# Two of seven quarter products as wide products, and a tail with seeded banks: one change to a two-layer decoder trunk on Trainium2

## The chip, the cores and the metric

The kernel runs on one core of one Trainium2 chip. The metric is the device time of one execution in microseconds; less is better. The profile names the engines PE (TensorE, matrix products), PEld (its weight loads), DVE (VectorE), ACT (ScalarE), POOL (GpSimd) and SP (SyncE, which mainly issues DMAs).

## The reference

Two decoder layers over 512 tokens of width 1024, all in float32. Layer 0 mixes tokens with a gated delta rule, layer 1 with sliding-window attention; both also read 256 memory tokens, and both end with a feed-forward part. The change lies in that part and in the last norm:

```python
D_MODEL = 1024; SEQ = 512; DEPTH = 2; D_FF = 2816

def rms_norm(x, g):
    return x * rsqrt(mean(x * x, axis=-1) + EPS) * g

def swiglu(h, w_gate_up, w_down):
    gu = h @ w_gate_up                       # 1024 -> 2 x 2816
    return (silu(gu[..., :D_FF]) * gu[..., D_FF:]) @ w_down

for layer in range(DEPTH):
    ...                                      # token mixing, memory attention, w_out
    x = x + swiglu(rms_norm(x, ln_ffn[layer]), w_gate_up[layer], w_down[layer])
    ...
return rms_norm(x, ln_final)
```

## The kernel before, in words

Activations lie transposed in SBUF: a tile holds 128 features by 512 tokens, and the residual stream is the eight tiles `x[0]` to `x[7]`. Every float32 product is made of three fp32r matmuls: each operand is split into a rounded part (hi) and the rest (lo), and `mm3` adds wh·ah, wh·al and wl·ah in one PSUM bank. `split` makes the parts: ACT copies hi (`whi<-wraw`, `h<-x`), DVE subtracts (lo). `pair` allocates the two parts of an activation, `h` and `l`, as two tiles. A bank holds 128 x 512 floats, and `banks` deals the eight banks out by tag.

A tile scheduler walks the program in the order in which it is written and puts each instruction into the queue of its engine; each queue runs in order, and semaphores order the queues among each other. The generator `quarters` is advanced step by step by `begin` and `end`, so that the pieces of neighbouring pairs interleave.

**The feed-forward part.** `ffn` does the 22 gate and 22 up columns of 128 features in two halves of 11. Column 0 of each half, and gates 1 and 2 of the first half, are plain products 512 tokens wide. All others go in pairs through `quarters`: 19 pairs in each layer, 38 in all. A pair of columns is a 2 x 2 block matrix (two columns by two halves of the 1024 input features), the input another (two halves of the features by two halves of 256 tokens), and Strassen's scheme in Winograd's form makes the four output blocks of seven products in place of eight. Each product sums over four steps (512 features), each of three matmuls 256 tokens wide.

The products are called here by the input that they read. 11 reads the first feature half of the first 256 tokens, 21 and 22 the second feature half of the first and of the last 256 tokens, straight from the parts of `h`; t1 to t4 read sums that `token_sums` has made once. PE's order in a pair is 11, t1, t4 of the pair before, t2, 21, 22, t3. The banks are `pa`, `pb` and `pc`, of which 256 columns each are used: `pa` gathers 11, t2 (their sum is called u2) and t3 and t4 behind it; `pb` holds 21, `pc` t1 and on top of it 22. What is wanted between, ACT copies out of PSUM by `held` into `fs`: p1 (product 11), p5 (t1) and u2. DVE adds 21 to p1 and 22 to u2. Each product's weight quarter (`wraw` by DMA; the sums `ws`, of which s1 is one, by a DMA and an accumulating DMA of POOL) is split just before it is needed into a ring of six places (`ring`: three buffers of `whi` and `wlo`, two halves each).

**The down projection** follows each half: for m = 0 to 7 it sums eleven steps into a bank `pj`, and DVE adds that to `x[m]`.

**The tail** is the end of layer 1: output tiles m = 6 and m = 7 of the last down projection, each in two parts of 256 tokens. PE's order is m6a, m7a, m6b, m7b (a the first 256 tokens, b the last). After each product `add` puts it on `x[m]` by DVE and ACT squares the result into `sq`; `final` sums the squares over the features with matmuls by `ones` and takes the reciprocal root by ACT, once for a part; `store` scales the output tiles `T` by it and sends them off. Ahead of the products' results, ACT copies tiles 0 to 5 times their gain into `T` for both parts, twelve scalings of 128 x 256.

Of the kernel before, what the change touches and what calls it, by code (L numbers as in the profile page):

```python
# [18 lines left out]
P = 128  # L19
# [64 lines left out]
    return c  # L84


class Builder:
    def __init__(self, tc, a):
        self.tc, self.nc, self.a = tc, tc.nc, a
# [71 lines left out]

    def pair(self, pool, tag=None, bufs=None):
        if tag is None:
            tag, bufs = "", KD
        return tuple(self.t(pool, [P, T], F32R, tag + p, bufs) for p in "hl")


    def split(self, src, hi, lo, eng=None):
# [27 lines left out]
    def mm3(self, ps, w, k, act, start, stop, more=False):  # L196

        (wh, wl), (ah, al) = w, act
        s = slice(k * P, (k + 1) * P)
        self.head = self.mm(ps, wh[:, s], ah, start, False, more)  # L200
        self.mm(ps, wh[:, s], al, False, False, more)
        self.last = self.mm(ps, wl[:, s], ah, False, stop, more)

    def project(self, src, acts, tag="pj", order=range(KD), w=None):
        steps = self.projected(src, acts, tag, order, w)
# [38 lines left out]
    def build(self):  # L244
        tc, nc, a = self.tc, self.nc, self.a
        with ExitStack() as st:
            opened = lambda name, **kw: tc.tile_pool(name=name, bufs=1, reuse_waits="tile", **kw)
            pool = lambda name, **kw: st.enter_context(opened(name, **kw))
            cp = pool("const")
            self.wpool, self.apool = pool("w"), pool("acta")  # L250
            self.dpool = pool("scratch", space=DRAM)
            self.load_constants(cp)
            self.weng = nc.vector
            with opened("layer0", side="right") as self.mpool:
                with self.banks(pj=3, g=2, sc=3):
# [10 lines left out]
            with opened("ffn0", side="right") as fp, self.banks(pj=2, g=6):  # L266
                self.ffn(fp, xp, 0, h, self.apool, rope=True)
            with self.banks(pj=2, qk=2, pt=2), opened("swa", side="right") as sp:
                h = self.output(xp, 1, *self.swa(sp))
            with opened("ffn1", side="right") as fp, self.banks(pj=2, g=6):  # L270
                self.ffn(fp, xp, 1, h, self.bpool)

    def load_constants(self, cp):
# [820 lines left out]
    def ffn(self, fp, xp, layer, h, apool, rope=False):  # L1094
# [6 lines left out]
        col = lambda f, up: a["wgu"][layer, 2 * f + up]  # L1101

        def gate(f, up=()):
            ps = self.project(col(f, 0), h, "pj")
# [54 lines left out]
        for f0 in (0, half):  # L1159
            acts.clear()  # L1160
            places.clear()
            up = self.projected(col(f0, 1), h, "g")
            g = gate(f0, up)
            u = self.t(fp, [P, T], F32, "fu", 3)
            self.tt(nc.vector, u, list(up)[-1], g, ALU.mult)
            put(u)
            for f in range(f0 + 1, f0 + half, 2):
                if f == 1:
                    g = []
                    for i in range(2):  # L1170
                        for _ in range(2 - i):
                            sums.append(self.token_sums(fp, layer, len(sums), h))
                        g.append(gate(f + i))
                    sums.append(self.token_sums(fp, layer, len(sums), h))
                else:
                    g = begin(f, 0, (self.rstd, self.rstd), "fg", 4, lambda x: self.fn(x, x, AF.Silu))
                begin(f, 1, g, "fu", 3, put)
            end()
            self.acc = self.floor if layer else None
            tail = KD - 2 if f0 and layer else KD  # L1180
            down = lambda m, j, n, **kw: self.weight(a["wdn"][layer, m][:, (f0 + j) * P:(f0 + j + n) * P], **kw)
            for m in range(tail):
                if layer and f0 == 0:
                    self.tt(nc.vector, self.x[m], self.x[m], self.root, ALU.mult)
                ps = self.bank("pj")
                for j, n in ((0, 6), (6, 5)):
                    w = down(m, j, n)
                    for k in range(n):
                        self.mm3(ps, w, k, acts[j + k], j + k == 0, j + k == half - 1)
                add(self.x[m], ps)  # L1190
                if f0:
                    self.acc = self.accumulate(xp, self.acc, self.x[m], m)
                if rope and f0 == 0 and m == 0:
                    self.rope_tables(fp)
        if tail < KD:
# [9 lines left out]
            for t in parts:  # L1205
                acc = self.acc[:, t]
                for m in range(tail, KD):
                    ps = self.bank("pj")[:, t]
                    for k in range(half):
                        self.mm3(ps, w[m][k // 6], k % 6, [x[:, t] for x in acts[k]], k == 0, k == half - 1)  # L1210
                    x = self.x[m][:, t]
                    add(x, ps)
                    sq = self.t(fp, [P, T], F32, "fg", 4)[:, t]
                    self.square(sq, x)
                    if m < KD - 1:
                        self.copy(outs[len(ends)][1][:, m % 4, :], x, scale=self.gain(G_FIN, m))
# [3 lines left out]
                ends.append(self.final(fp, (acc, sq), t))  # L1220
            for n, ((ps, r), o, t) in enumerate(zip(ends, outs, parts)):
                self.store(ps, r, o, t, n)

    def token_sums(self, fp, layer, j, h):

# [19 lines left out]
        hl = self.weight(None, raw=raw, pool=fp, tags=("T", "T"), bufs=8)  # L1245
        parts = {f"t{i + 1}": [x[:, i * q:(i + 1) * q] for x in hl] for i in range(4)}
        parts["11"] = [x[:, :q] for x in h[j]]
        parts["21"], parts["22"] = ([x[:, i * q:(i + 1) * q] for x in h[j + 4]] for i in range(2))
        return parts

    def quarters(self, fp, src, sums, by, u, ring):
# [13 lines left out]
        ins = nc.sync.dma_start(last, a22).ins  # L1265
        if self.behind is not None:
            self.nosync(ins, self.behind)
        pa, pb, pc = (self.bank("g")[:, :q] for _ in range(3))

        def product(ps, raw, b, first):  # L1270

# [5 lines left out]
        def held(ps):  # L1277
            o = self.t(fp, [P, q], F32, "fs", 3)
            self.copy(o, ps)
            return o  # L1280

        product(pa, a1[:, :T], "11", True)
        p1 = held(pa)
        self.held = self.copied
        product(pc, s1, "t1", True)
        p5 = held(pc)
        yield

        self.tt(nc.vector, a1[:, :T], s1, a1[:, :T], ALU.add)
        product(pa, a1[:, :T], "t2", False)  # L1290
        u2 = held(pa)
        product(pb, a1[:, T:], "21", True)
        self.tt(nc.vector, u[0][:, :q], pb, p1, ALU.add)
        self.tt(nc.vector, a1[:, T:], a1[:, :T], a1[:, T:], ALU.add)
        product(pc, a1[:, T:], "22", False)
        self.tt(nc.vector, u[0][:, q:], pc, u2, ALU.add)
        self.tt(nc.vector, u[0], u[0], by[0], ALU.mult)
        product(pa, s3, "t3", False)
        self.stt(u[1][:, q:], pa, -1.0, p5, ALU.mult, ALU.subtract)
# [12 lines left out]

    def rstd_from(self, acc, *parts, after, root=None):
        self.use(LN_EXP)
        ps = self.bank("pt" if "pt" in self.pbufs else "g")
        self.sum_parts(ps, acc, *parts, after)
        if root is None:
            self.rsqrt(self.rstd, ps, D)
# [168 lines left out]
    def final(self, fp, squares, t):  # L1487

        self.use(ROOT)
        ps, to = (self.bank("g")[:, t] for _ in range(2))  # L1490
        for k, sq in enumerate(squares):
            self.mm(ps, self.ones, sq, k == 0, k == len(squares) - 1)
        r = self.t(fp, [P, T], F32, "ws", 4)[:, t]
# [1 line left out]
            self.fn(o, ps, AF.Abs_reciprocal_sqrt, scale=1.0 / D)  # L1495
        return to, r

    def store(self, ps, r, o, t, part):

        nc = self.nc  # L1500
        rows = self.a["out"][part]
# [1 line left out]
        wide = lambda f, n: f.unsqueeze(1).to_broadcast([P, n, t.stop - t.start])  # L1503
        send = lambda k, n, by=nc.sync: by.dma_start(rows[:, k:k + n, :], some(k, n))
        self.tt(nc.gpsimd, some(0, 2), some(0, 2), wide(r, 2), ALU.mult)
        for k, n in ((2, 2), (4, 3)):
            self.tt(nc.vector, some(k, n), some(k, n), wide(ps, n), ALU.mult)
            send(k, n)
        self.stt(some(7, 1)[:, 0, :], self.x[7][:, t], self.gain(G_FIN, 7), ps, ALU.mult, ALU.mult)
        send(7, 1)  # L1510
        send(0, 2, nc.scalar if part else nc.sync)


# [62 lines left out]
```

## Time and profile before

| | |
|---|---|
| runs | 1138.91, 1139.19, 1139.49 us; median 1139.19 |
| the profiled execution | 1139.24 us; its span from the first to the last instruction 1137.2 us |
| PE busy | 1127.4 us, 99% of the span, 7337 matmuls |
| DVE busy | 829.0 us, 73% |
| ACT busy | 634.1 us, 56% |
| POOL busy | 72.8 us, 6% |
| mean granted TensorE clock | 0.999 |

Busy shares are means over stages with different limits, and an engine with free time delays nothing unless something waits for it. In rows of the order of time the columns are start, length, engine, line, operation, tiles and shapes, with a wait and what ended it in brackets; "x4" at the end stands for four in a row.

### The profile page before, as it was taken

The page shows a single profiled execution, that of the slowest core. Times are in us where ns is not written, and L with a number is a line of the kernel's source. Part 1 is how long each engine was busy: PE and PEld are TensorE (multiplying, and loading weights), DVE is VectorE, ACT ScalarE, POOL GpSimd, SP SyncE. Part 2 cuts the span into 40 slices and gives each one's busy share as a digit, 9 for nine tenths or more (in the row PEclk, how much of TensorE's full clock was granted, in tenths as well). Part 3 has the DMA queues.
Part 4 walks back from the last instruction along what each step waited for, and adds up shares of the span by engine and source line. Part 5 has one row for each costly group of instructions (what it writes and reads, how often), then busy time and mean ns, then how long its engine had stood idle before and what let it go on. Part 6 is the DMA issues. An engine that isn't in the chain of part 4 may idle for free.

```text
span 1137.2 us, 19289 instructions
## 1 busy us (share of the span) xinstructions
PE 1127.4 (99%) x7337; PEld 991.3 (87%) x7337; DVE 829.0 (73%) x1542; ACT 634.1 (56%) x1271; POOL 72.8 (6%) x89
## 2 busy tenths in 40 slices
PE   9999999999999999999999999999999999999997
PEld 8888778887899988899988887788999988999986
DVE  7676976577888975588955877839999533889543
ACT  8588664566566632366643555956666322666433
POOL 0000000000011001011000000000112000111000
PEclk9999999999999999999999999999999999999999
DMA  8344352244677536378433421116677533776232
GB/s 312 116 145 149 93 130 85 84 121 148 172 163 187 142 108 176 106 178 200 126 89 101 130 74 38 56 39 194 142 203 182 141 100 105 171 191 154 78 101 86
DMA packets 71536, 151.14 MB, mean 133 GB/s; under 512 B 16861, under 2 KB 17141, under 8 KB 71445
## 3 DMA queue, kind: packets, MB, share of 16 engines
q1 hardware_dynamic: 60164, 129.21, 36.7%
q0 software_dynamic: 11136, 20.45, 11.5%
q8 instruction: 57, 0.93, 0.3%
q14 instruction: 35, 0.28, 0.1%
q10 hardware_dynamic: 144, 0.26, 0.1%
HBM read 142.94 MB, written 6.96 MB: 132 GB/s over the span
## 4 chain that ended last, share of the span: by engine, by line
PE 95%; DVE 2%; ACT 1%; DMA 1%; issue 0%; DVEq 0%; SPq 0%; ACTq 0%
PE pj L146 45%; PE g L146 38%; PE sc L146 6%; PE qk L146 3%; PE pt L146 2%; PE pt L150 1%; PE g L150 1%; DVE big L153 1%; ACT T L140 0%; DVE wlo L153 0%; DVE qv L156 0%; DVE btmp L153 0%; DMA early<-in_early 0%; ACT sm L134 0%; DMA wraw<-in_wdn 0%
## 5 line engine op out<-in xcount | busy, mean ns | idle before, releaser
L140 ACT ACTIVATE whi<-wraw 128x512 fp32r<-128x512 f32 (+3 forms) x318 | 235.9, 749 | 253.5 <-PE pj L146 167.6
L153 DVE TENSOR_TENSOR wlo<-wraw,whi 128x512 fp32r<-128x512 f32 (+3 forms) x318 | 263.3, 838 | 92.4 <-ACT whi L140 84.8
L146 PE MATMUL pj<-h,whi 128*128 128x512 f32 (+1 forms) x652 | 256.4, 395 | 0.0
L146 PE MATMUL pj<-l,whi 128*128 128x512 f32 (+1 forms) x652 | 254.4, 390 | 0.0
L146 PE MATMUL pj<-h,wlo 128*128 128x512 f32 (+1 forms) x652 | 254.1, 390 | 0.0
L146 PE MATMUL g<-T,whi 128*128 128x256 f32 x1216 | 218.5, 280 | 0.0
L146 PEld LDWEIGHTS g<-T,whi 128*128 128x128 f32 x1216 | 186.1, 188 | 1.2 <-DVE fu L156 1.2
L146 PE MATMUL g<-T,wlo 128*128 128x256 f32 x608 | 170.1, 280 | 0.0
L146 PEld LDWEIGHTS pj<-h,whi 128*128 128x128 f32 x652 | 122.4, 188 | 28.2 <-issue 4.1
L146 PE MATMUL g<-h,wlo 128*128 128x256 f32 (+1 forms) x500 | 146.1, 292 | 0.0
L146 PE MATMUL g<-l,whi 128*128 128x256 f32 (+1 forms) x500 | 146.0, 292 | 0.0
L146 PE MATMUL g<-h,whi 128*128 128x256 f32 (+1 forms) x500 | 145.6, 291 | 0.0
L146 PEld LDWEIGHTS pj<-h,wlo 128*128 128x128 f32 x652 | 122.5, 188 | 25.3 <-issue 0.9
L146 PEld LDWEIGHTS pj<-l,whi 128*128 128x128 f32 x652 | 122.8, 188 | 24.0 <-DVE l L1444 0.3
L146 PEld LDWEIGHTS g<-T,wlo 128*128 128x128 f32 x608 | 114.3, 188 | 0.0
L146 PEld LDWEIGHTS g<-l,whi 128*128 128x128 f32 x500 | 95.0, 190 | 2.0
L146 PEld LDWEIGHTS g<-h,whi 128*128 128x128 f32 x500 | 94.9, 190 | 2.0
L146 PEld LDWEIGHTS g<-h,wlo 128*128 128x128 f32 x500 | 95.1, 190 | 1.7
L1262 POOL DMA_DIRECT2D ws<-in_wgu x38 | 33.5, 881 | 741.2 <-DMA ws<-in_wgu 584.6
L140 ACT ACTIVATE whi<-ws 128x512 fp32r<-128x512 f32 x76 | 48.0, 632 | 47.1 <-PE g L146 37.8
L153 DVE TENSOR_TENSOR wlo<-ws,whi 128x512 fp32r<-128x512 f32 x76 | 52.1, 685 | 6.9 <-ACT whi L140 6.8
L1263 POOL DMA_DIRECT2D ws<-in_wgu x38 | 34.4, 906 | 194.4 <-DVE wlo L153 92.2
(399 smaller groups left out, 1681.4 us busy)
## 6 DMA issues: line engine op xcount, KB each, us to landing
wraw<-in_wgu SPq DMA_DIRECT2D x50, 512.0 KB, 4.2
ws<-in_wgu SPq DMA_DIRECT2D x76, 256.0 KB, 3.4
ws<-in_wgu POOLq DMA_DIRECT2D x76, 256.0 KB, 4.8
wraw<-in_win SPq DMA_DIRECT2D x26, 512.0 KB, 3.7
wraw<-in_wdn SPq DMA_DIRECT2D x32, 384.0 KB, 3.1
wraw<-in_wdn SPq DMA_DIRECT2D x32, 320.0 KB, 2.9
wraw<-in_wgu SPq DMA_DIRECT2D x38, 256.0 KB, 4.4
wraw<-in_wout SPq DMA_DIRECT2D x16, 512.0 KB, 3.5
```

Source lines behind the costliest of these rows:

```text
L140: self.copied = self.nc.scalar.activation(out, in_, AF.Copy, **kw).ins
L146: return self.nc.tensor.matmul(out, lhsT, rhs, start=start, stop=stop, skip_group_check=more).ins
L150: return self.nc.tensor.transpose(out, in_, self.ident[:k, :k]).ins
L153: return eng.tensor_tensor(out=out, in0=a, in1=b, op=op).ins
L1262: nc.gpsimd.dma_start(s1, a22, accum_op=ALU.add)
L1263: nc.gpsimd.dma_start(s3, a21, accum_op=ALU.add)
```

## The change

It has three parts.

*The operands.* `pair` allocates both parts of an activation as one tile `hl` of 128 x 2 x 512; `both` is that tile. A new `wide` makes a step of two matmuls: wh times both parts, 256 tokens of each, 512 columns in all, into a whole bank, whose lower half (columns 0 to 255) takes wh·ah and whose upper half wh·al; and wl·ah, 256 columns, into the lower or first half. In the diff `ps[:, :q]` is the first half, and `ps[:, q:]` the second, the low parts' half; the text calls the sum in it the low half. `wide` never starts a bank, it adds to what lies there.

*The pairs.* Products 21 and 22 become wide (`seeded`). What a bank holds before is put there by ACT. `clear` writes zeros (a constant times 0) into the first half of `pc` and the second half of `pb`; product 11 is copied from `pa` into the first half of `pb`, and u2 into the second half of `pc`, in place of the copies p1 and u2 into SBUF. t1 is added to the cleared half of `pc`. After each wide product ACT copies its second half out to `fs`, and DVE adds it to the first. The banks are dealt `pj=2, g=2, pb=2, pc=2` in place of `pj=2, g=6`; gates 1 and 2, the first up column and the second part's `final` take theirs from `pb` and `pc`.

*The tail.* m6a, m7a and m6b become wide: ACT copies `x[m]` into the bank's own half (a seed) and clears the low half ahead of the product; behind it ACT copies the low half out and DVE adds the two into `x[m]`. m7b stays narrow with x as its seed, and its square and its scaling read PSUM; `add` falls away there. For the last part `store` scales tile 7 by its gain beforehand, on ACT, and sends tiles (2,2), (4,2), (6,2), (0,2) in place of (2,2), (4,3), (7,1), (0,2), first tile and count.

```diff
     def pair(self, pool, tag=None, bufs=None):
         if tag is None:
-            tag, bufs = "", KD
-        return tuple(self.t(pool, [P, T], F32R, tag + p, bufs) for p in "hl")
+            tag, bufs = "hl", KD
+        both = self.t(pool, [P, 2, T], F32R, tag, bufs)
+        hl = Pair((both[:, 0, :], both[:, 1, :]))
+        hl.both = both
+        return hl
...
+    def wide(self, ps, w, k, both, stop):
+        (wh, wl), q = w, T // 2
+        s = slice(k * P, (k + 1) * P)
+        self.mm(ps.rearrange("p (a t) -> p a t", a=2), wh[:, s], both, False, False, True)
+        self.last = self.mm(ps[:, :q], wl[:, s], both[:, 0, :], False, stop, True)
+
+    def clear(self, ps):
+        zero = self.ones.unsqueeze(1).to_broadcast([P, ps.shape[1] // P, P])
+        self.copy(ps.rearrange("p (a t) -> p a t", t=P), zero, scale=0.0)
...
-            with opened("ffn1", side="right") as fp, self.banks(pj=2, g=6):
+            with opened("ffn1", side="right") as fp, self.banks(pj=2, g=2, pb=2, pc=2):
...
                 for m in range(tail, KD):
-                    ps = self.bank("pj")[:, t]
-                    for k in range(half):
-                        self.mm3(ps, w[m][k // 6], k % 6, [x[:, t] for x in acts[k]], k == 0, k == half - 1)
-                    x = self.x[m][:, t]
-                    add(x, ps)
+                    bank, x = self.bank("pj"), self.x[m][:, t]
+                    own, low = (bank[:, i * T // 2:(i + 1) * T // 2] for i in range(2))
                     sq = self.t(fp, [P, T], F32, "fg", 4)[:, t]
+                    self.copy(own, x)
+                    if t.start and m == KD - 1:
+                        x = own
+                        for k in range(half):
+                            self.mm3(own, w[m][k // 6], k % 6, [a[:, t] for a in acts[k]], False, k == half - 1, True)
+                    else:
+                        self.clear(low)
+                        for k in range(half):
+                            self.wide(bank, w[m][k // 6], k % 6, acts[k].both[:, :, t], k == half - 1)
+                        self.copy(sq, low)
+                        self.tt(nc.vector, x, own, sq, ALU.add)
                     self.square(sq, x)
...
-        parts["21"], parts["22"] = ([x[:, i * q:(i + 1) * q] for x in h[j + 4]] for i in range(2))
+        parts["21"], parts["22"] = (h[j + 4].both[:, :, i * q:(i + 1) * q] for i in range(2))
...
-        pa, pb, pc = (self.bank("g")[:, :q] for _ in range(3))
+        pa, pb, pc = self.bank("g")[:, :q], self.bank("pb"), self.bank("pc")
+        self.clear(pc[:, :q])
+        self.clear(pb[:, q:])
...
+        def seeded(ps, raw, b):
+            w = ring()
+            self.split(raw, *w)
+            for j in range(4):
+                self.wide(ps, w, j, sums[j][b], j == 3)
+            return held(ps[:, q:])
+
         product(pa, a1[:, :T], "11", True)
-        p1 = held(pa)
+        self.copy(pb[:, :q], pa)
         self.held = self.copied
-        product(pc, s1, "t1", True)
-        p5 = held(pc)
+        product(pc[:, :q], s1, "t1", False)
+        p5 = held(pc[:, :q])
         yield
 
         self.tt(nc.vector, a1[:, :T], s1, a1[:, :T], ALU.add)
         product(pa, a1[:, :T], "t2", False)
-        u2 = held(pa)
-        product(pb, a1[:, T:], "21", True)
-        self.tt(nc.vector, u[0][:, :q], pb, p1, ALU.add)
+        self.copy(pc[:, q:], pa)
+        low = seeded(pb, a1[:, T:], "21")
+        self.tt(nc.vector, u[0][:, :q], pb[:, :q], low, ALU.add)
         self.tt(nc.vector, a1[:, T:], a1[:, :T], a1[:, T:], ALU.add)
-        product(pc, a1[:, T:], "22", False)
-        self.tt(nc.vector, u[0][:, q:], pc, u2, ALU.add)
+        low = seeded(pc, a1[:, T:], "22")
+        self.tt(nc.vector, u[0][:, q:], pc[:, :q], low, ALU.add)
```

In `store`, with the tail's `x` and the part's slice `t` handed in:

```diff
-        for k, n in ((2, 2), (4, 3)):
+        if t.start:
+            self.copy(some(7, 1)[:, 0, :], x, scale=self.gain(G_FIN, 7))
+        for k, n in ((2, 2), (4, 2), (6, 2 if t.start else 1)):
             self.tt(nc.vector, some(k, n), some(k, n), wide(ps, n), ALU.mult)
-            send(k, n)
-        self.stt(some(7, 1)[:, 0, :], self.x[7][:, t], self.gain(G_FIN, 7), ps, ALU.mult, ALU.mult)
-        send(7, 1)
+            if k < 6:
+                send(k, n)
+        if not t.start:
+            self.stt(some(7, 1)[:, 0, :], x, self.gain(G_FIN, 7), ps, ALU.mult, ALU.mult)
+        send(6, 2)
```

The scheduler gives these queues. PE in product 21 of a pair of layer 0, before; the numbers behind the names are tile numbers, `g_3795` is `pb` and each `h`, `l` couple one step's input:

```order
L146 MATMUL g_3795<-h_2934,whi_3279 128x256
L146 MATMUL g_3795<-l_2935,whi_3279 128x256
L146 MATMUL g_3795<-h_2934,wlo_3280 128x256
L146 MATMUL g_3795<-h_2974,whi_3279 128x256
L146 MATMUL g_3795<-l_2975,whi_3279 128x256
L146 MATMUL g_3795<-h_2974,wlo_3280 128x256
```

The same place after:

```order
L150 MATMUL pb_3750<-hl_2914,whi_3256 128x512
L150 MATMUL pb_3750<-hl_2914,wlo_3257 128x256
L150 MATMUL pb_3750<-hl_2953,whi_3256 128x512
L150 MATMUL pb_3750<-hl_2953,wlo_3257 128x256
L150 MATMUL pc_3751<-hl_2914,whi_3258 128x512
```

The steps three and four stand in the same form and are left out, and the last row is the first of 22. Two rows for a step take the place of three, and the order of the products is the same.

ACT in a pair of layer 0, before, from the split of the next pair's s1 (`ws_3915`) on; `wraw_3792` holds this pair's weights for t4 and `wraw_3913` the next pair's for 11, t2, 21 and 22, `fs_3861<-g_3794` is the held copy of u2, `fg` a silu, and `h<-fu` the split of a finished column:

```order
L140 ACTIVATE whi_3283<-ws_3915 128x512
L134 ACTIVATE fg_3648<-fg_3648 128x512
L140 ACTIVATE whi_3279<-wraw_3792 128x512
L140 ACTIVATE fs_3861<-g_3794 128x256
L140 ACTIVATE whi_3279<-wraw_3913 128x512
L140 ACTIVATE whi_3281<-wraw_3913 128x512
L140 ACTIVATE h_3973<-fu_3782 128x512
L140 ACTIVATE whi_3283<-ws_3916 128x512
```

ACT in such a pair after, again from the split of the next pair's s1 on:

```order
L144 ACTIVATE whi_3260<-ws_3741 128x512
L144 ACTIVATE hl_3674<-fu_3484 128x512
L144 ACTIVATE whi_3260<-wraw_3618 128x512
L144 ACTIVATE pc_3622<-g_3620 128x256
L144 ACTIVATE whi_3256<-wraw_3739 128x512
L144 ACTIVATE fs_3703<-pb_3621 128x256
L144 ACTIVATE whi_3256<-wraw_3739 128x512
L144 ACTIVATE fs_3717<-pc_3622 128x256
L144 ACTIVATE pb_3875<-ones_69 128x256
L144 ACTIVATE pc_3876<-ones_69 128x256
```

In both, the copy of u2 (`fs_3861<-g_3794`, then `pc_3622<-g_3620`) stands right behind the split for t4 (`whi<-wraw_3792`, then `whi<-wraw_3618`). New are the two copies of low halves behind the wide products and the two clears of banks of a later pair.

ACT in the tail before; `T<-x` are scalings (the last of the twelve first), `fg<-x` squares, and `g_11774` the reciprocal root of the first part:

```order
L140 ACTIVATE T_11682<-x_521_2729,gains_67 128x256
L140 ACTIVATE T_11682<-x_522_2730,gains_67 128x256
L143 ACTIVATE fg_11730<-x_523_2731 128x256
L140 ACTIVATE T_11680<-x_523_2731,gains_67 128x256
L143 ACTIVATE fg_11770<-x_524_2732 128x256
L134 ACTIVATE g_11774<-g_11773 128x256
```

The same place after; `pj_11443` is the bank of m6a, `pj_11475` that of m7a and `pj_11512` that of m6b:

```order
L144 ACTIVATE T_11430<-x_505_2713,gains_67 128x256
L144 ACTIVATE T_11430<-x_506_2714,gains_67 128x256
L144 ACTIVATE fg_11444<-pj_11443 128x256
L144 ACTIVATE pj_11475<-x_508_2716 128x256
L144 ACTIVATE pj_11475<-ones_69 128x256
L147 ACTIVATE fg_11444<-x_507_2715 128x256
L144 ACTIVATE T_11428<-x_507_2715,gains_67 128x256
L144 ACTIVATE pj_11512<-x_507_2715 128x256
L144 ACTIVATE pj_11512<-ones_69 128x256
L144 ACTIVATE fg_11476<-pj_11475 128x256
```

The seed and the clear of m7a, and those of m6b, stand behind the twelve scalings and behind the copy of m6a's low half; those of m6a stand further ahead in the queue, before the last splits of weights.

More of the change, by code (lines that the diff above doesn't have):

```diff
@@ L84, in constants @@
     return c
+class Pair(tuple):
+    pass
 class Builder:
@@ L265, in build @@
                     h = self.output(xp, 0, mix)
-            with opened("ffn0", side="right") as fp, self.banks(pj=2, g=6):
+            with opened("ffn0", side="right") as fp, self.banks(pj=2, g=2, pb=2, pc=2):
                 self.ffn(fp, xp, 0, h, self.apool, rope=True)
@@ L1103, in gate @@
         def gate(f, up=()):
-            ps = self.project(col(f, 0), h, "pj")
+            ps = self.project(col(f, 0), h, {1: "pb", 2: "pc"}.get(f, "pj"))
             if f == 0:
@@ L1161, in ffn @@
             places.clear()
-            up = self.projected(col(f0, 1), h, "g")
+            up = self.projected(col(f0, 1), h, "pb")
             g = gate(f0, up)
@@ L1219, in ffn @@
                         acc = nxt
-                ends.append(self.final(fp, (acc, sq), t))
-            for n, ((ps, r), o, t) in enumerate(zip(ends, outs, parts)):
-                self.store(ps, r, o, t, n)
+                ends.append((x, *self.final(fp, (acc, sq), t)))
+            for n, (end, o, t) in enumerate(zip(ends, outs, parts)):
+                self.store(*end, o, t, n)
     def token_sums(self, fp, layer, j, h):
@@ L1314, in rstd_from @@
         self.use(LN_EXP)
-        ps = self.bank("pt" if "pt" in self.pbufs else "g")
+        ps = self.bank("pt" if "pt" in self.pbufs else "pc")
         self.sum_parts(ps, acc, *parts, after)
@@ L1489, in final @@
         self.use(ROOT)
-        ps, to = (self.bank("g")[:, t] for _ in range(2))
+        ps, to = (self.bank(tag)[:, t] for tag in (("pb", "pc") if t.start else ("g", "g")))
         for k, sq in enumerate(squares):
@@ L1496, in final, with store @@
         return to, r
-    def store(self, ps, r, o, t, part):
+    def store(self, x, ps, r, o, t, part):
         nc = self.nc
```

## The prediction

> **What bounds the kernel now.** I read the page first, then the busy times by stage, then the chain of waits, and last the order of time in one column pair and in the tail. The page says which engine to count:
>
> ```profile
> span 1137.2 us, 19289 instructions
> ...
> PE 1127.4 (99%) x7337; PEld 991.3 (87%) x7337; DVE 829.0 (73%) x1542; ACT 634.1 (56%) x1271; POOL 72.8 (6%) x89
> ```
>
> PE is busy throughout. The busy times by stage (microseconds, then PE, PEld, DVE, ACT, POOL) show two stretches of column pairs and the tail:
>
> ```profile
> 318.70:407.00 88.30, 88.30 (x746) 88.26 (x746) 77.38 (x139) 54.48 (x105) 11.82 (x14) 1.00 0.67 162
> ...
> 961.00:1064.50 103.50, 103.50 (x854) 102.55 (x853) 88.14 (x157) 64.13 (x122) 13.97 (x16) 1.00 0.61 148
> ...
> 1109.00:1137.20 28.20, 20.36 (x151) 18.80 (x149) 9.85 (x17) 10.25 (x25) 2.56 (x2) 0.95 0.24 87
> ```
>
> In the column pairs PE never waits, ACT has 38% of the time free and DVE some 13%. There a shorter PE stream is worth its whole length, and added ACT work is free until PE has to wait for it. In the tail the other engines show. The chain of waits (start, length, what) gives the length of the streams:
>
> ```profile
> 772.47 16.32 PE pj L146 x72
> ...
> 805.62 88.06 PE g L146 x744
> ...
> 1113.69 4.79 ACT T L140 x12
> ```
>
> A 512-column matmul takes 16.32 / 72 = 0.2267 us from start to start, a 256-column one 88.06 / 744 = 0.1184. [...] The last row is the one outside PE that matters: twelve ACT operations in a row.
>
> **Part 1, the wide step.** The products with h as input are a little slower than that mean. This is PE in order of time, from the start of product t2 over 21 and 22 to the start of t3:
>
> ```profile
> 522.00 0.40 PE L146 MATMUL g<-T,whi 128*128 128x256 f32 x2
> ...
> 523.41 0.28 PE L146 MATMUL g<-h,whi 128*128 128x256 f32 x1
> ...
> 526.28 0.40 PE L146 MATMUL g<-T,whi 128*128 128x256 f32 x2
> ```
>
> t2 takes 1.41 us for its 12 matmuls (0.1175 each), 21 and 22 together 2.87 us for 24 (0.1196). The row of 744 is four sevenths T products and three sevenths h products; with 0.1175 for the T ones it gives 0.1195 for h. A wide step replaces two of these by one of 512: 2 x 0.1195 - 0.2267 = 0.012 us saved. The number of pairs is in the page, as the adds into s1:
>
> ```profile
> L1262 POOL DMA_DIRECT2D ws<-in_wgu x38 | 33.5, 881 | 741.2 <-DMA ws<-in_wgu 584.6
> ```
>
> 38 pairs x 2 products x 4 steps = 304 steps, so 304 x 0.012 = 3.65 us less. No row here has a moving operand in two runs of 256. Its price is bounded by the 0.2267 of contiguous operands and by the 0.239 of two separate ones, which gains nothing; I take 0.2267, the same columns in one instruction. [...]
>
> **Part 2, ACT in a pair.** Three copies out of PSUM become five, and two clears come on top; the nearest row is the copies of before (busy, mean ns):
>
> ```profile
> L140 ACT ACTIVATE fs<-g 128x256 f32<-128x256 f32 x114 | 41.8, 366 | 0.7 <-PE g L146 0.6
> ```
>
> 4 x 0.366 = 1.5 us more per pair, against 38% free of the 9.9 us that seven products take, 3.8 us: hidden. DVE gets no operation more, but its two adds for 21 and 22 now wait for ACT's copy of the low half (0.37 us and a hand-over of about 0.05) instead of PE. Weight splits run several products ahead of PE in a ring of six places, and DVE has 13% of 9.9 us, 1.3 us, to spare; I put this at nothing. If that cover were gone, each add would cost PE up to 0.4 us.
>
> The one tight wait is u2. It must now lie in the upper half of pc before 22 starts, and in ACT's queue the split of the weight for t4 stands ahead of it. Before has that queue order in every second pair:
>
> ```profile
> 513.24 0.63 ACT L134 ACTIVATE fg<-fg 128x512 f32<-128x512 f32 x1 [0.41 <-DVE fg L156]
> 513.78 0.61 ACT L140 ACTIVATE whi<-wraw 128x512 fp32r<-128x512 f32 x1
> 514.30 0.37 ACT L140 ACTIVATE fs<-g 128x256 f32<-128x256 f32 x1
> ...
> 513.47 0.28 PE L146 MATMUL g<-h,whi 128*128 128x256 f32 x1
> ```
>
> The copy ends at 514.67, 1.20 us after 21 began. A wide 21 lasts 4 x (0.2267 + 0.1195) = 1.38 us, so 22 would find u2 with 0.18 us to spare, 0.13 after the hand-over. In the changed order the silu ahead has its DVE operation before a 512-wide sum, not behind it, which gives up to 0.3 us more. Cost: nothing, with a thin margin.
>
> **Part 3, the tail.** Here the change adds a wait. The four products are m6a, m7a, m6b, m7b. PE and then ACT around the first two:
>
> ```profile
> 1111.17 0.28 PE L146 MATMUL pj<-h,whi 128*128 128x256 f32 x1
> ...
> 1115.11 0.28 PE L146 MATMUL pj<-h,T 128*128 128x256 f32 x1
> ...
> 1119.31 0.70 PE L146 MATMUL g<-sqa,ones 128*128 128x256 f32 x2
> ...
> 1112.43 0.74 ACT L140 ACTIVATE T<-wraw 128x640 fp32r<-128x640 f32 x1 [2.92 <-DMA wraw<-in_wdn]
> 1113.08 0.62 ACT L143 ACTIVATE sq<-x 128x512 f32<-128x512 f32 x1
> 1113.60 4.89 ACT L140 ACTIVATE T<-x,gains 128x256 f32<-128x256 f32 x12
> 1118.39 0.40 ACT L143 ACTIVATE fg<-x 128x256 f32<-128x256 f32 x1
> ```
>
> Before, m7a starts at 1115.11, right behind m6a, and needs nothing of ACT but its weights. Now its first matmul waits until ACT has put x into the bank and cleared the low half. The seeds of m6a stand ahead of the last splits, where ACT waits for DMA and PE anyway (2.92 us idle): free. Those of m7a stand behind the twelve scalings, which wait for the weight's DMA (1112.43) and end their turn at 1118.39, and behind the copy of m6a's low half. From there: copy 0.27 (the turn of a 256-wide copy is shorter than its 0.37, as is that of a 512-wide one: 513.78 to 514.30), seed 0.40, clear 0.40 and behind the seed by a wait on the same bank, hand-over 0.05: with 0.02 between them, 1119.53. The prices of writing PSUM are not in the trace; between 0.27 and 0.50 each they move this by 0.3 us.
>
> Wide, m6a ends at 1111.17 + 11 x 0.348 = 1115.0, and PE then stands still for 4.5 us. m7a starts 1119.53 - 1115.11 = 4.42 later than before. Against it: m7a is 0.11 shorter; the 0.25 us by which the sum of squares at 1119.31 was late is gone, as that work is now done while m7a runs; m6b is 0.11 shorter and waits 0.06 for m7a's squares, whose chain has a copy more. At the start of m7b the tail is 4.42 - 0.11 - 0.25 - 0.11 + 0.06 = 4.0 us late.
>
> m7b is seeded and stays narrow, and its end is read by ACT from PSUM. Before, DVE's add stood there:
>
> ```profile
> 1128.35 0.42 DVE L153 TENSOR_TENSOR x<-pj,x 128x256 f32<-128x256 f32 x1 [2.62 <-PE pj L146]
> 1128.81 0.42 ACT L143 ACTIVATE fg<-x 128x256 f32<-128x256 f32 x1 [3.13 <-DVE x L153]
> 1129.28 0.70 PE L146 MATMUL g<-fg,ones 128*128 128x256 f32 x2 [0.53 <-ACT fg L143]
> ...
> 1130.42 1.55 DVE L153 TENSOR_TENSOR T<-T,g 128x512 f32<-128x512 f32 x2 [1.64 <-ACT g L134]
> 1131.89 0.48 DVE L156 SCALAR_TENSOR_TENSOR T<-x,gains,g 128x256 f32<-128x256 f32 x1
> ```
>
> Square instead of add saves 1128.81 - 1128.35 = 0.5 us. The three scalings behind it become equal 512-wide ones and end about where the two and the 256-wide one did (1132.37); the last DMA is 256 KB instead of 128, the sum of bytes the same: 0 to 0.2 us, taken as 0. Tail: +4.0 - 0.5 = +3.5 us.
>
> **The sum.** Against the profiled execution's own 1139.24 us (span 1137.2 and 2.0 around it; the median of the runs is 0.05 lower): -3.65 + 3.5 = -0.15, so 1139.1 us. Two terms of opposite sign nearly cancel. No change that a measurement of this kernel can tell begins at 0.2%, 2.3 us.
>
> **The rivals.**
>
> *The wide step gains nothing.* Place: the moving operand in two runs. Against it speak the steady 0.2267 rows; for it, that no row shows such an operand. Each ns of the 12 is worth 0.3 us; with nothing gained it is 1139.24 + 3.5 = 1142.7, slower, and it decides from under 4 ns. Chance 0.15, half of it beyond the bound.
>
> *The u2 copy comes too late.* Place: ACT's queue between t2 and 22, margin 0.13 to 0.4 us. If DVE, now waiting for ACT, hands over the silu's or the split's input later than that, PE waits in each of 38 pairs; 0.2 us each are 7.6 us: 1146.7, slower. Against it: DVE's spare time, and the ring. Chance 0.10.
>
> *The clock falls in the tail's gap.* The granted clock (next to last columns) and the start of the program:
>
> ```profile
> 1130.00:1134.30 4.30, 0.00 (x0) 0.00 (x0) 1.94 (x3) 0.66 (x2) 1.26 (x1) 1.00 0.50 191
> 1134.30:1137.17 2.87, 0.00 (x0) 0.00 (x0) 0.00 (x0) 0.00 (x0) 0.00 (x0) 0.50 0.23 79
> ...
> 1.19 3.51 PE L146 MATMUL g<-wabs 128*128 128x256 f32 x15 [1.19 <-DVE eps L292]
> 4.54 0.28 PE L146 MATMUL pj<-mh,whi 128*128 128x256 f32 x1
> ```
>
> Behind the last matmul the clock held 4.3 us and then fell to half; the new gap is 4.5 us. The program's first 15 narrow matmuls took (4.54 - 1.19) / 15 = 0.223 us each, half speed, for 3.3 us. If m7a had to start so, it would lose half of up to 3.3 us, some 1.5: 1140.6, still no change to be told. Chance 0.15. [...]
>
> *The seeds do not hold PE.* If ACT were through earlier, m7a would start at 1115.0, and the squares of m6a, behind a copy more, would hold PE some 1.0 us longer than now: tail +1.0 - 0.1 - 0.5 = +0.4, total 1136.0, faster. Against it stands the queue, in which nothing can pass the twelve scalings; for it, that these start when a DMA of 3 us lands. Chance 0.12.
>
> **How the numbers follow.** The forecast has 0.45, the clock 0.15, the seeds 0.12, the wide step 0.15, u2 0.10, and 0.03 are for a wait I don't see. Faster by over 0.2% is the seeds' case: 0.12. Slower is half of the wide step's, u2 and the rest: 0.20. The rest, 0.68, is within. The range leaves out the seeds' case and u2's: from 1136.6 to 1142.8, where the upper end holds a wide step that gains nothing.
>
> **What would show it.** Right: 512-column matmuls from hl into pb and pc at 0.227 us from start to start and a stretch of pairs without PE waits, about 1.8 us shorter per layer; in the tail one PE gap of 4 to 4.6 us before pj<-hl,T, ended by ACT's write of pj; no DVE add before the last square. Wrong: steps of hl at over 0.35 us, PE waits for pc in each pair, or a tail whose two seeds come before the scalings.

## The result and the profile after

The changed kernel is slower: 1144.49 us median of six runs (1143.09 to 1144.85) against 1139.24 (1138.91 to 1139.49), a ratio of 1.0045, 95% interval 1.0032 to 1.0058. The forecast was 1139.1, at most 1142.8. The profiled execution took 1144.19 us. Its page:

```profile
span 1142.4 us, 18802 instructions
...
PE 1128.6 (99%) x7000; PEld 976.4 (85%) x7000; DVE 820.8 (72%) x1542; ACT 678.8 (59%) x1434; POOL 72.8 (6%) x89
```

PE has 337 matmuls fewer than before (304 in the pairs, 33 in the tail) and is busy 1.2 us longer; the span is 5.2 us longer. The tail is where that lies. The end of the chain of waits (start, length, what), and then PE's waits by what ended them (total, times, longest):

```profile
1066.56 40.71 PE pj L150 x178
1114.87 2.88 ACT T L144 x7
1118.77 6.44 PE pj L150 x22
```

```profile
PE pj L150 <- ACT pj L144: 4.0, 1, 4.0
...
PE pc L150 <- ACT pc L144: 0.6, 2, 0.3
```

The tail in order of time, PE's last matmul of m6a and m7a first, then ACT:

```profile
1114.52 0.28 PE L150 MATMUL pj<-ac,wlo 128*128 128x256 f32 x1
...
1118.77 5.38 PE L150 MATMUL pj<-hl,T 128*128 128x512 f32 x16 [3.97 <-ACT pj L144]
...
1112.88 4.88 ACT L144 ACTIVATE T<-x,gains 128x256 f32<-128x256 f32 x12
...
1117.66 0.36 ACT L144 ACTIVATE fg<-pj 128x256 f32<-128x256 f32 x1
1117.92 0.37 ACT L144 ACTIVATE pj<-x 128x256 f32<-128x256 f32 x1
1118.33 0.39 ACT L144 ACTIVATE pj<-ones 128x256 f32<-128x256 f32 x1
```

The forecast gap is there: copy, seed and clear of m7a stand behind the twelve scalings, and PE starts m7a at 1118.77. What was not forecast is the 6.44 us that m7a then takes. The busy times by stage, with the granted clock in the third column from the right:

```profile
1117.00:1118.00 1.00, 0.00 (x0) 0.00 (x0) 0.00 (x0) 1.00 (x4) 0.00 (x0) 0.52 0.00 0
1118.00:1123.00 5.00, 4.24 (x13) 3.65 (x14) 0.85 (x2) 2.07 (x7) 0.00 (x0) 0.50 0.00 0
1123.00:1124.00 1.00, 1.00 (x5) 0.81 (x5) 0.00 (x0) 0.00 (x0) 0.00 (x0) 0.56 0.00 0
1124.00:1126.00 2.00, 2.00 (x13) 1.77 (x12) 0.34 (x1) 0.38 (x1) 0.00 (x0) 1.00 0.00 0
```

The clock fell about 2.2 us after the last matmul of m6a and came back at 1123.9, when most of m7a was done.

In the pairs the wide matmuls gave less than forecast. The first matmuls of 21, t3, 11, t1 and of the next 21, in order of time:

```profile
522.85 0.39 PE L150 MATMUL pb<-hl,whi 128*128 128x512 f32 x1
...
525.65 0.40 PE L150 MATMUL g<-T,whi 128*128 128x256 f32 x2
527.09 0.40 PE L150 MATMUL g<-hl,whi 128*128 128x256 f32 x2
528.52 0.40 PE L150 MATMUL pc<-T,whi 128*128 128x256 f32 x2
...
532.75 0.39 PE L150 MATMUL pb<-hl,whi 128*128 128x512 f32 x1
```

A pair takes 9.90 us, where 523.41 to 533.34, the start of 21 to that of the next, was 9.93 before. 21 and 22 fell from 2.87 to 2.80, but t3 and 11 rose by some 0.02 and 0.01.

And the last pair of each layer has a wait. ACT and then PE there:

```profile
1058.59 0.63 ACT L138 ACTIVATE fg<-fg 128x512 f32<-128x512 f32 x1 [1.09 <-DVE fg L160]
1059.24 1.28 ACT L129 ACT_TABLE_LOAD   x1
1060.54 0.37 ACT L144 ACTIVATE pc<-g 128x256 f32<-128x256 f32 x1
...
1060.38 0.28 PE L150 MATMUL pb<-hl,wlo 128*128 128x256 f32 x1
1060.96 0.50 PE L150 MATMUL pc<-hl,whi 128*128 128x512 f32 x1 [0.30 <-ACT pc L144]
```

A table load stands between the last silu and the copy of u2. 21 begins at 1059.09 there and 22 1.87 us later, 0.47 more than in the other pairs, and 22 takes 0.10 more.

### The profile page after: what moved, and what is told of

It reads as the page before. It is cut to its first block, busy times and chain, and to the rows that moved or that the text cites. A ratio compares the mean times of both kernels' runs of the same rounds, so it can differ in the third digit from the quotient of the medians.

```text
span 1142.4 us, 18802 instructions
## 1 busy us (share of the span) xinstructions
PE 1128.6 (99%) x7000; PEld 976.4 (85%) x7000; DVE 820.8 (72%) x1542; ACT 678.8 (59%) x1434; POOL 72.8 (6%) x89
## 4 chain that ended last, share of the span: by engine, by line
PE 95%; DVE 2%; ACT 1%; DMA 1%; issue 1%; DVEq 0%; SPq 0%; ACTq 0%
PE pj L150 43%; PE g L150 22%; PE pc L150 10%; PE pb L150 7%; PE sc L150 6%; PE qk L150 3%; PE pt L150 2%; PE pt L154 1%; PE g L154 1%; DVE big L157 1%; ACT T L144 0%; DVE wlo L157 0%; DVE qv L160 0%; DVE btmp L157 0%; DMA early<-in_early 0%
## 5 line engine op out<-in xcount | busy, mean ns | idle before, releaser
L150 PE MATMUL pj<-hl,whi 128*128 128x512 f32 x1224 | 389.9, 396 | 0.0
L150 PEld LDWEIGHTS pj<-hl,whi 128*128 128x128 f32 x1224 | 226.6, 188 | 50.2 <-issue 4.3
L150 PE MATMUL pj<-hl,wlo 128*128 128x512 f32 (+1 forms) x620 | 241.5, 390 | 0.0
L150 PEld LDWEIGHTS pj<-hl,wlo 128*128 128x128 f32 x620 | 116.5, 188 | 24.0 <-issue 0.9
L150 PE MATMUL pb<-hl,whi 128*128 128x512 f32 x248 | 84.6, 394 | 0.0
L150 PE MATMUL pc<-hl,whi 128*128 128x512 f32 x184 | 65.3, 397 | 0.6 <-ACT pc L144 0.6
L150 PE MATMUL g<-hl,whi 128*128 128x256 f32 (+1 forms) x328 | 63.5, 290 | 0.0
L150 PE MATMUL pb<-hl,wlo 128*128 128x256 f32 (+1 forms) x200 | 61.3, 307 | 0.0
L150 PE MATMUL pj<-ac,whi 128*128 128x512 f32 x186 | 58.8, 396 | 0.0
L150 PE MATMUL pc<-T,whi 128*128 128x256 f32 x304 | 55.4, 280 | 0.0
```

Source lines behind the costliest of these rows:

```text
L150: return self.nc.tensor.matmul(out, lhsT, rhs, start=start, stop=stop, skip_group_check=more).ins
```

## The experiments

Ten kernels ran. Times are medians; the kernel before, run beside them, had 1139.3 to 1139.4.

**The pairs alone.** The changed kernel with the tail and the store of before:

```diff
-                    self.copy(own, x)
-                    ...
-                            self.wide(bank, w[m][k // 6], k % 6, acts[k].both[:, :, t], k == half - 1)
+                    for k in range(half):
+                        self.mm3(ps, w[m][k // 6], k % 6, [x[:, t] for x in acts[k]], k == 0, k == half - 1)
+                    x = self.x[m][:, t]
+                    add(x, ps)
```

> The column pairs as in the changed kernel, the tail and the store as before. Theory (the trace of the changed kernel): a pair takes 9.90 us in place of 9.93, 1.3 us less over 38 pairs, and the last pair of each layer gives 0.5 us back in a wait for u2 behind a table load: 1138.9 us, 0.3 less than before, with matmuls of 512 columns from hl at about 0.235 us. Rival (the pairs carry half of what was lost): 1141 to 1142 us.

1138.53 us, ratio 0.9993 (0.9984 to 1.0002): 0.8 below before, by medians, and not distinguishable from no change.

**The tail alone.** The kernel before with `wide`, `clear`, the joint tiles, and the tail and the store of the changed kernel, the reverse of that diff.

> The tail and the store of the changed kernel, the column pairs as before. Theory: one PE gap of some 4 us ahead of m7a, m7a at half clock, and the whole loss is here: 1139.2 + 5.6 = 1144.8 us. Rival (half of the loss belongs to the pairs): 1141.5 us.

1145.23 us, ratio 1.0052 (1.0037 to 1.0066). The whole loss is in the tail: +5.9 here and -0.8 above make the +5.2 of both. Its m7a in order of time and by stage:

```profile
1119.11 4.61 PE L150 MATMUL pj<-hl,T 128*128 128x512 f32 x16 [4.11 <-ACT pj L144]
```

```profile
1119.70:1123.10 3.40, 3.40 (x13) 2.84 (x12) 0.14 (x1) 0.74 (x3) 0.00 (x0) 0.51 0.00 0
```

In this execution the clock fell only after m7a had begun, and was low for 3.4 us.

**A filled gap.** To part the gap from the clock, PE got work that needs nothing of ACT:

```diff
+                        if m == KD - 1:
+                            ps = self.bank("pc")
+                            for k in range(WARM):       # 19
+                                self.mm(ps, w[m - 1][0][0][:, :P], acts[0][0], k == 0, k == WARM - 1)
                         self.clear(low)
```

> The changed kernel with 19 matmuls of 512 columns between m6a and m7a, into a bank that nothing reads; they need nothing of ACT and last 19 x 0.227 = 4.3 us, 0.3 past the end of the gap. Theory (PE's idle time lets the clock fall, and the fall costs 2.5 us on top of the gap): granted clock 1.00 throughout m7a, m7a in 3.9 us, 1142.3 us. Rival (m7a is slow for another reason, such as ACT's work in PSUM): m7a still 6.3 us, 1144.8 us.

1142.03 us, ratio 1.0024 (1.0015 to 1.0034). The chain of waits shows the filling and m7a, and the stage its clock:

```profile
1114.90 4.31 PE pc L153 x19
1119.21 3.87 PE pj L153 x22
```

```profile
1119.00:1123.00 4.00, 4.00 (x24) 3.51 (x24) 0.43 (x1) 1.31 (x4) 0.00 (x0) 1.00 0.02 4
```

m7a starts 0.4 us later than in the changed kernel, but takes 3.87 us in place of 6.44. The fall of the clock is the idle time's, and it costs 2.5 us by the medians; work without use is faster here than none.

**A half-filled gap.** The same with 9 matmuls.

> The changed kernel with 9 matmuls of 512 columns between m6a and m7a, 2.0 us: they end 2.2 us before m7a can start, so that half of PE's gap is left. Theory (the clock falls only after more than 2.2 us without a matmul; the shortest seen is 2.3, the longest 4.8): granted clock 1.00 throughout m7a, 1142.0 us as with the gap filled. Rival (any gap of some 2 us lowers it, or work at a low share does): m7a at half clock in part, 1143 to 1144.5 us.

1143.25 us, ratio 1.0030 (1.0019 to 1.0041). The rival was right. m7a's first row, and the gap and what follows by stage:

```profile
1118.92 4.61 PE L153 MATMUL pj<-hl,T 128*128 128x512 f32 x16 [2.07 <-ACT pj L147]
```

```profile
1116.85:1118.92 2.07, 0.00 (x2) 0.00 (x1) 0.42 (x1) 2.04 (x7) 0.00 (x0) 1.00 0.00 0
...
1119.30:1122.60 3.30, 3.30 (x13) 2.81 (x11) 0.36 (x1) 0.96 (x3) 0.00 (x0) 0.50 0.00 0
```

A gap of 2.07 us was enough, and by the medians the fall cost 1.2 us here. The runs spread from 1141.64, as with the gap filled, to 1143.54, so it depends on the execution; the section on the prediction gives the likely reason.

**The seeds ahead.** In the tail of the changed kernel the same instructions in another order; the lines left out seed the second part's banks in the loop:

```diff
-            for o, t in zip(outs, parts):
-                for k in range(tail):
-                    self.copy(o[k // 4][:, k % 4, :], self.x[k][:, t], scale=self.gain(G_FIN, k))
+            for m in range(tail, KD):
+                seed(parts[0], m)          # copy x, clear the low half
+            scalings(3)
...
+                    if not t.start:
+                        seed(parts[1], m)
+                        scalings(3 if m < KD - 1 else 6)
```

> The changed kernel with another order of ACT's queue in the tail alone: both seeds and clears of the first part ahead of the twelve scalings, those of the second part as soon as their banks are free, three or six scalings at a time between. Theory (the loss is the place of the seeds behind the scalings): no PE gap over 0.5 us before m7a, clock 1.00, the tail some 0.5 to 1 us shorter than before: 1138.0 to 1138.5 us. Rival (copies, clears and adds of the wide products cost the tail by themselves): 1139.5 to 1141 us.

1137.62 us, ratio 0.9986 (0.9977 to 0.9996). PE runs without a stop into m7a:

```profile
1066.38 52.13 PE pj L150 x238
1120.79 6.51 PE pj L150 x48
```

From m6a's first matmul (1110.61) to the end of the span (1135.7) the tail takes 25.1 us; before it took 26.0, in the changed kernel 31.6. Seeds and wide products cost the tail nothing; their place in ACT's queue did.

**A contiguous operand.** Why does a wide step save less than 12 ns? This kernel has only the changed pairs:

```diff
-        self.mm(ps.rearrange("p (a t) -> p a t", a=2), wh[:, s], both, False, False, True)
+        self.mm(ps, wh[:, s], self.whole[id(both)], False, False, True)   # hi of all tokens
```

> As the kernel with the changed pairs alone, but the wide matmuls of products 21 and 22 read 512 columns that lie together (the hi part of all tokens) in place of two runs of 256 (hi and lo of one half): this leaves out the low part of those products. Theory (the wide step saves 7.5 ns and not 12 because its operand lies in two runs): the 512-column matmul falls from 0.235 to 0.227 us, a pair from 9.90 to 9.83, the time by 38 x 0.067 = 2.5 us to 1136.0. Rival (it is the change between matmuls of 512 and 256 columns): pitch, pair and time as with the changed pairs alone, 1138.5 us.

1138.28 us, ratio 0.9992 (0.9983 to 1.0001), and the pair is unchanged, 532.85 - 522.95 = 9.90:

```profile
522.95 0.39 PE L151 MATMUL pb<-hl,whi 128*128 128x512 f32 x1
...
532.85 0.39 PE L151 MATMUL pb<-hl,whi 128*128 128x512 f32 x1
```

The two runs of the operand cost nothing here, which was the prediction's only doubt about the wide step.

**No clears.** From the changed pairs alone, the two `clear` lines removed, `t1` with `start=True`, and the first step of 21 split:

```diff
-        self.clear(pc[:, :q])
-        self.clear(pb[:, q:])
...
+                    self.mm(ps[:, :q], w[0][:, :P], x[:, 0, :], False, False, True)
+                    self.mm(ps[:, q:], w[0][:, :P], x[:, 1, :], True, False, True)
+                    self.mm(ps[:, :q], w[1][:, :P], x[:, 0, :], False, False, True)
```

> As the kernel with the changed pairs alone, without ACT's two clears in each pair: t1 starts its half of pc itself, and the first step of 21 is three narrow matmuls of which the second starts its half of pb. Theory (t3 and 11 are 0.03 us slower in a pair because ACT then writes to PSUM): t3 back to 1.41, pair 9.88, 1137.7 us. Rival (those products are slower for a reason of PE's own): t3 at 1.43, pair 9.91, 1138.8 us.

1139.55 us, ratio 1.0001 (0.9992 to 1.0010). The output of this kernel is off by a relative 0.92, so only its time is read. t3 fell to 1.41 us, but t1 rose to 1.43 from 1.41 and t4 and t2 together to 2.85 from 2.82, and the pair stayed at 9.90 to 9.91; by the mean of 34 pairs it is 9.92. This tells nothing of the clears: it moved the place of a slower product.

**Narrow matmuls on the filled banks.** The wide instruction alone undone, all else kept:

```diff
-                self.wide(ps, w, j, sums[j][b], j == 3)
+                self.mm(ps[:, :q], w[0][:, s], x[:, 0, :], False, False, True)
+                self.mm(ps[:, q:], w[0][:, s], x[:, 1, :], False, False, True)
+                self.mm(ps[:, :q], w[1][:, s], x[:, 0, :], False, j == 3, True)
```

> As the kernel with the changed pairs alone, but products 21 and 22 as three matmuls of 256 columns a step, into the same two halves of the same filled banks: all copies, clears and waits of the change stay, the wide instruction alone is gone. Theory (the slower t3 and 11 belong to the work around the banks): 21 and 22 together 2.87, t3 and 11 still 0.03 slower, pair 9.96, and the waits at the table loads stay: 1141.5 us. Rival (the slower t3 and 11 belong to the wide matmuls ahead of them): pair 9.93, 1140.4 us.

1140.32 us, ratio 1.0008 (0.9999 to 1.0017): the rival's number. 21 of one pair, then 21, t3, 11 and t1 of the next:

```profile
513.85 0.40 PE L150 MATMUL pb<-hl,whi 128*128 128x256 f32 x2
...
523.78 0.40 PE L150 MATMUL pb<-hl,whi 128*128 128x256 f32 x2
...
526.65 0.40 PE L150 MATMUL g<-T,whi 128*128 128x256 f32 x2
528.06 0.40 PE L150 MATMUL g<-hl,whi 128*128 128x256 f32 x2
529.48 0.40 PE L150 MATMUL pc<-T,whi 128*128 128x256 f32 x2
```

The pair is 9.93, t3 1.41 and 11 1.42 as before. So ACT's added copies and clears cost PE nothing inside a pair, and the slower t3 and 11 come with the wide matmuls ahead of them.

**The table load behind u2**, on top of the reordered tail:

```diff
         self.copy(pc[:, q:], pa)
+        self.table_users.append(self.copied)
```

> The kernel with ACT's tail in another order, and the table load put behind every copy of u2 in ACT's queue. Theory (in the last pair of each layer 22 waits for u2 behind a table load of 1.28 us, 0.47 and 0.10 us there): the waits go, 2 x 0.57 = 1.1 us less than the reordered tail alone: 1136.5 us. Rival (what now stands behind the table load makes PE wait as long): 1137.6 us.

1136.62 us, ratio 0.9973 (0.9963 to 0.9984). The last pair now:

```profile
1058.23 0.39 PE L150 MATMUL pb<-hl,whi 128*128 128x512 f32 x1
...
1059.62 0.40 PE L150 MATMUL pc<-hl,whi 128*128 128x512 f32 x1
...
1059.06 0.37 ACT L144 ACTIVATE pc<-g 128x256 f32<-128x256 f32 x1
1059.44 1.28 ACT L129 ACT_TABLE_LOAD   x1
```

22 follows 21 after 1.39 us, and PE's wait for `pc` is gone: 1.0 us less than with the reordered tail alone.

**Fewer changes of size**, on top of that: the same matmuls, in 21 the four with low weights first, in 22 last:

```diff
...
+            steps = lows + wides if b == "21" else wides + lows
+            for n, (o, x, y) in enumerate(steps):
...
+                self.last = self.mm(o, x, y, False, n == 7, True)
```

> The kernel with both mends, and in products 21 and 22 another order of the same matmuls: in 21 the four narrow ones with the low weights first and then the four wide ones, in 22 the four wide ones and then the four narrow ones, so that a pair changes between 512 and 256 columns 2 times and not 16 times. Theory (each change of size costs; contiguous wide matmuls take 0.227 and narrow ones 0.1195): 21 and 22 together 8 x 0.227 + 8 x 0.1195 = 2.77 in place of 2.80, pair 9.87, 38 x 0.03 = 1.2 us less: 1135.4 us; and 1134.3 if t3 and 11 are no longer 0.03 slower. Rival (the wide matmul into a filled bank is slow by itself): pair 9.90, 1136.6 us.

1135.54 us, ratio 0.9966 (0.9954 to 0.9979), the fastest of all, 0.34% faster than before. 21, 22, t3, 11 and the next 21:

```profile
522.87 0.64 PE L150 MATMUL pb<-hl,wlo 128*128 128x256 f32 x4
524.27 1.07 PE L150 MATMUL pc<-hl,whi 128*128 128x512 f32 x4
525.66 0.40 PE L150 MATMUL g<-T,whi 128*128 128x256 f32 x2
527.07 0.40 PE L150 MATMUL g<-hl,whi 128*128 128x256 f32 x2
...
532.72 0.63 PE L150 MATMUL pb<-hl,wlo 128*128 128x256 f32 x4
```

This pair takes 9.85 us, one of the shorter ones; the mean of 34 is 9.87, where it was 9.90 in the kernel of the run before. Over 38 pairs that is 1.1 us, the difference of the two medians: the order alone brought it, and the theory's number came true. Its place did not. 21 and 22 together take 2.80 us by the mean of 34 pairs, where 2.77 was expected and 2.81 stood before, although equal sizes now lie side by side. The gain is in what follows: t3, from its row to that of 11, is back at 1.41, and t3 and 11 take 0.03 us less together. That the order of sizes matters to the products behind is thereby shown; that each change of size costs by itself is not, and why a wide step takes 0.350 us stays open.

## Why the prediction was wrong

Its sum had two terms that nearly cancelled. Against the traces (pairs: 38 times the difference of a pair, 9.940 before and 9.898 after by the mean of the 34 that have another pair behind them; gap: what the tail lost beyond the clock's 2.5; tail: from m6a's first matmul to the end):

| term | forecast | measured |
|---|---|---|
| wide steps | -3.65 us | -1.6 us |
| u2's copy | 0 | +1.1 us |
| tail, the gap | +3.5 us | +3.1 us |
| tail, the clock | 0 | +2.5 us |
| sum | -0.15 us | +5.1 us (span: +5.2) |

**The wide step, part 1: right in kind, mis-sized.** It was priced by rows of streams with one size, 0.2267 and 0.1195. In a stream that changes size at every matmul a step of the two takes 1.40 / 4 = 0.350 us, where the sum of those rows is 0.346 and three narrow ones took 0.3585: 8 ns saved, not 12. And the two products behind, t3 and 11, take 0.02 us more in a pair. The failed step is the price "0.2267, the same columns in one instruction": 304 steps and their followers saved 1.6 us in place of 3.65. Equal sizes side by side did not bring the step down to 0.346 either. The rival for this step doubted the wrong thing, the operand in two runs; its price of nothing gained was too far the other way.

**u2's copy, part 2: the rival held in 2 pairs of 38.** The margin of 0.13 to 0.4 us was worked out for a pair in the middle, and there it is enough. The last pair of a layer has other work in ACT's queue, and the trace of before showed it. These rows were there to be read, a silu, the table load, and the copy of u2:

```profile
1059.26 0.63 ACT L134 ACTIVATE fg<-fg 128x512 f32<-128x512 f32 x1 [1.03 <-DVE fg L156]
1059.91 1.28 ACT L125 ACT_TABLE_LOAD   x1
1061.20 0.39 ACT L140 ACTIVATE fs<-g 128x256 f32<-128x256 f32 x1
```

Before, nobody but DVE waited for that copy; the change put PE behind it. The failed step is "Cost: nothing, with a thin margin", taken from one pair for all.

**The tail's gap, part 3: right.** m7a was forecast to start at 1119.53 and started at 1118.77, with the work in the order given; the gap is 4.0 us where 4.5 was forecast. (For m6a a step was taken at 0.348, where part 1 has 0.346; that moves the gap by 0.02.) That the seeds would not hold PE, the fast rival, is refuted by the same rows, and the run with the seeds ahead shows that their place was the cause.

**The clock: the step that failed by most.** It was a rival at 0.15, for 1.5 us, "if m7a had to start so". It was the case: m7a took 2.57 us more than with the gap filled (6.44 against 3.87). Two things were misread. The 4.3 us that the clock had held behind the program's last matmul were taken as the time that it takes to fall, and one execution does not show that: here it held 2.2 us, in the tail alone about 4.7, in the half-filled gap 2.5. And the loss was cut to part of the program's first 3.3 us at half speed (0.223 us a matmul), while the clock came back here only after 5.1 us of m7a.

What sets the length of a fall the traces do not name; they give its times. The clock was low for 3.41 us in the tail alone (1119.73 to 1123.15) and in the half-filled gap (1119.31 to 1122.73), and for 6.83 us, twice that, in the changed kernel (1117.05 to 1123.87), where it was then full for 13.65 us, four times that, until 1137.53. From its first rise to its first fall it was full for 1112.75 us there (4.30 to 1117.05), 326 times 3.4133, and for 1129.81 us in the kernel before (4.50 to 1134.31), 331 times. The clock also fell where PE had not stood still for a whole such stretch: with the gap of 2.07 us it had been at work for 1.34 of the 3.41 us ahead of the fall.

What went with a fall shows when the twelve traces are laid side by side. Count windows of 3.413 us from the first rise of the clock; every fall stands at the end of one. PE's busy time, the first number behind the comma, in the window ahead of the fall in the half-filled gap, in the fullest window that ended in a fall (the end of the run with the seeds ahead), and in the emptiest that did not (the end of the run with the table load moved):

```profile
1115.90:1119.31 3.41, 1.34 (x7) 0.81 (x6) 0.50 (x2) 3.38 (x11) 0.00 (x0) 1.00 0.00 0
...
1126.80:1130.21 3.41, 1.63 (x9) 0.83 (x7) 1.30 (x3) 1.41 (x4) 0.96 (x1) 1.00 0.00 0
...
1125.26:1128.67 3.41, 1.95 (x11) 1.15 (x10) 0.98 (x2) 1.41 (x4) 0.64 (x1) 1.00 0.00 0
```

From full speed the clock fell behind every window with PE busy for up to 1.63 of the 3.41 us (48%) and behind none with 1.95 (57%) or more; between them no window lay. So in these traces not the length of a gap counted but how much of it lay in one window, and 1.78 us, 3.41 less 1.63, were enough. By an estimate from these rows a gap of over 3.6 us, twice 1.78, holds that much of one window wherever it begins. By that estimate the forecast gap of 4.5 us made the fall all but certain, where the prediction had 0.15, its author's estimate; with 2.07 us it is a matter of where the window begins.

**The chances.** Slower by over 0.2% had 0.20. The rivals were priced one at a time; three of them came together in part (the wide step, u2, the clock), and the sum of the three left the range, whose upper end held one of them alone.

## What to carry to other kernels

When a change makes PE wait for an engine that it did not wait for, read that engine's queue at every place where the wait will stand, the last turn of the loop and its table loads (1.28 us here) above all, not in one turn of the middle. A gap on PE of 2.07 us cost the clock here, and those of 3.97 and 4.11 us did; such a gap is priced with that, here another 1.2 us for the first and 2.5 for the long one. Filling it took the clock's part away (1142.03 us in place of 1144.49), and moving the producer ahead of bulk work took both (1137.62). Price a new instruction mix by rows of such a mix, and with it the products behind: another order of the same matmuls was worth 1.1 us here.

## What was not expected of the hardware

- A stream that alternates 512 and 256 columns took 0.350 us for the two, where rows of streams with one size add up to 0.346, and took the same with four equal sizes side by side (2.80 us for 21 and 22); but twelve narrow matmuls of t3 took 1.43 us behind the alternating stream and 1.41 behind the other.
- An operand of two runs of 256 columns with 1 KB between them was as fast as 512 together: a pair of 9.90 us both ways.
- The clock fell 2.2 to 4.7 us after the last matmul, with a gap of 2.07 us when PE was at work again, and stayed low for 3.41 or 6.83 us. In twelve traces a window of 3.41 us with PE busy for 0 to 48% of it ended in a fall, and none with 57% or more did.
